# Product-key expert stage of a two-layer trunk: 0.9 dots a tile and less of the other tokens' top-k between the gathers' begin and the gates

## The chip, the cores and the metric

The kernel runs on one core of a Trainium2 chip. The metric is device time in microseconds (us) of one execution, from repeated runs: before the change the median of three is 1582.73 us (1582.06 to 1584.29). A profiled execution of the same kernel took 1584.51 us, of which the span from the first to the last instruction is 1582.6 us. Engines are named as in the profile: PE multiplies matrices, DVE and ACT work on vectors, POOL (GpSimd) here issues row gathers, and SP issues most weight transfers.

## What is computed

Two layers run one after the other on 256 tokens of width 1024. Each mixes tokens (convolution, windowed attention, spatial gating) and then retrieves experts; the change lies in the second part, which for one layer is this:

```python
q = (t @ w_pq).reshape(T, PEER_HEADS, 2, PEER_HALF)
s = jnp.einsum('thpk,hpnk->thpn', q, sub_keys, preferred_element_type=jnp.float32)
top_s, top_i = lax.top_k(s, PEER_TOPK)
...
best_s, best_pos = lax.top_k(cand_s.reshape(T, PEER_HEADS, PEER_TOPK * PEER_TOPK), PEER_TOPK)
experts = jnp.take_along_axis(...)
gate = jax.nn.softmax(best_s, axis=-1)
u = expert_down[experts]
act = jax.nn.gelu(jnp.einsum('td,thkd->thk', t, u, ...), approximate=False)
wgt = (gate * act).astype(t.dtype)
vv = expert_up[experts]
return jnp.einsum('thk,thkd->td', wgt, vv)
```

There are 8 heads with 16 picks each, so 128 picks a token, among 16384 experts in each of the two tables (down and up), float32 throughout. The scale and shift of each norm come from a modulation, a product of one vector with a 1024 by 6144 matrix for each layer.

## The kernel before

**Two ways for the tokens.** Most tokens (168 in layer 0, 160 in layer 1) are dense: they are multiplied with every expert, in 128 tiles of 128 experts, first all of the down table and then all of the up table. The gate values are put into a dense array and multiply the activations. The other tokens (88 and 96) are sparse: for pick slot k, one indirect DMA by POOL (a gather) fetches 128 rows of 4 KB, one to a partition, of the down table, and DVE forms the 128 dot products at once (`dot(k)`, line 1084). Later the same is done with the rows of the up table (`add_row`, line 1099).

**The down loop** (in `experts`, lines 1239 to 1347) is a loop over tiles i = 0 to 127; "T38" below is the tile i = 38 of one layer. A tile's matmuls (`chunk_mm`, line 357) are 16 on PE, and its weights are one transfer of 512 KB into one of seven `raw` buffers. Even tiles' transfers are issued from ACT's queue (kind "second"), the others from SP's. Fifteen tiles, from T4 on, are loaded ahead into parts of the array `arena` that `AHEAD_AT` lists. After its matmul such a part can be lent to gathers as a row buffer.

**Order.** From here on the instructions stand in the order in which the program writes them (manual_schedule), on each engine. An engine works through its own list in order, so an instruction whose data is missing holds up all that stands behind it. In each tile, behind the matmuls, the program writes: the use of gates, the gelu of the tile pair on ACT (line 1150), the gate factors on ACT (`factors`, lines 1117 to 1123), a one-hot comparison on DVE (`compare`, line 1107), and then what the change touches:

- `run_fill(budget)` runs pieces of the top-k on DVE, each with a cost that was written by hand. The queue `fills[1]` belongs to the half of the tokens that holds the sparse ones, and `fills[0]` to the other half. When `fills[1]` is done, its picks are known, and this tile is `begin`. Three tiles later the gathers start, two a tile.
- When `fills[0]` is done (its last piece of work is `gate`, lines 922 to 924), two tiles later `to_picks` lets PE transpose the result (line 934), ACT copies it (lines 939 to 942), and one tile after that DVE forms the remainder (line 943) and `compare` runs for the first two gate groups. The next tile is `start`: ACT's `factors` for both groups are written there. From `start + FLUSH` tiles on PE multiplies the groups (`gate_mm`, line 1133), spread up to tile 124.
- Dots are written from `begin + D_FIRST` on at a rate a tile: `DOT_SLOW` while pieces are left in `fills[0]`, `DOT_FAST` from then to `start`, `DOT_RATE` afterwards. A dot frees its row buffer, and the next gather is written at once behind it (`fetch`). As many gathers are open as there are row buffers.
- `run_aside` multiplies one chunk of the next modulation on DVE (line 227). Six such chunks wait in buffers from tile 19 on.

In words, `passing` holds the lent parts of `arena` which the activations of later tiles will overwrite. Once `fills[0]` is down to `RETIRE` pieces they are not lent again.

Of the kernel before, what the change touches and what calls it, by code (L numbers as in the profile page):

```python
# [46 lines left out]
WHERE_LAG = 3  # L47
SETS_LAG = 6
SETS_KNOWN = 22
D_FIRST = 8  # L50
DOT_SLOW = 0.3
DOT_RATE = (0.85, 0.92)
DOT_FAST = 1.6
RETIRE = 9
AHEAD_AT = (8, 12, 16, 36, 40, 44, 48, 52, 56, 60, 64, 68, 100, 28, 32)
KEPT = 100
FLUSH = 6
# [8 lines left out]
FILL_DOWN = (2.2, 2.1)  # L66
# [16 lines left out]
def hybrid_trunk(ctx: ExitStack, tc: tile.TileContext, x_in, c_in, vec_in, w_ada, w_in, w_out, w_pq,  # L83
# [45 lines left out]
    def region(at, *shape):  # L129
        n = 1  # L130
        for s in shape:
            n *= s
        v = flat[:, at:at + n]
        if len(shape) == 2:
            v = v.rearrange("p (a b) -> p a b", b=shape[1])
        elif len(shape) == 3:
            v = v.rearrange("p (a b c) -> p a b c", b=shape[1], c=shape[2])
        return v
# [78 lines left out]
    fills = deque(), deque()  # L217

    def run_fill(budget):
        Src.credit = min(budget, Src.credit + budget)  # L220
        while (fills[0] or fills[1]) and Src.credit > 0:
            cost, fn = (fills[1] or fills[0]).popleft()
            fn()
            Src.credit -= cost
# [63 lines left out]
    def run_aside(least=4):  # L288
        if Src.asides and Src.asides[0][0] <= Src.cast - least:
            Src.asides.popleft()[1]()  # L290
# [29 lines left out]
    for layer in range(DEPTH):  # L320
# [3 lines left out]
        if layer == 0:  # L324
# [5 lines left out]
            n = len(head)  # L330
# [677 lines left out]
    def experts(layer, rest):  # L1008
# [59 lines left out]
        def fetch():  # L1068
            while free and len(held) < min(2 * TS, known_to[0]) and quota[0] > 0:
                quota[0] -= 1  # L1070
                n = len(held)
                k = n % TS
                held[n] = free.popleft()
                nc.gpsimd.indirect_dma_start(  # L1074
                    out=held[n], out_offset=None, in_=rows if n >= TS else down_rows[:, :],
                    in_offset=bass.IndirectOffsetOnAxis(ap=R_WHERE[:, k:k + 1].bitcast(U32), axis=0))
# [144 lines left out]
        begin = None  # L1221
# [12 lines left out]
        for i in range(128):  # L1234
# [32 lines left out]
                known_to[0] = SETS[0][1]  # L1267
                fetch()
            if start is None:
                run_fill(FILL_DOWN[layer] if begin is None else FILL_DOWN[layer] - 1.2 * DOT_SLOW)  # L1270
            if known:
                known_at.append((i + PICKS_LAG, known.pop()))
                if begin is None:
                    begin = i
# [14 lines left out]
            elif start is not None and i >= start + FLUSH:  # L1289
# [3 lines left out]
                while sent < want and not waiting:  # L1293
                    waiting.append((sent, gate_mm(sent)))
                    sent += 1
                    make = True
            if not retired and begin is not None and len(fills[0]) <= RETIRE:
                retired.extend(passing)
                for row in [row for row in free if any(row is r for r in passing)]:
                    free.remove(row)  # L1300
            n = i - AHEAD_FIRST
            if 0 <= n < len(AHEAD_AT) and AHEAD_AT[n] >= 28:
                assert not retired
                free.append(region(AHEAD_AT[n] * S, D))
                if AHEAD_AT[n] != KEPT:
                    passing.append(free[-1])
                fetch()
            if begin is not None:
                if i == begin + SETS_LAG:
                    spread_rest()  # L1310
                if i == begin + SETS_KNOWN:
# [4 lines left out]
                    fetch()  # L1316
                if i >= begin + D_FIRST:
                    due += DOT_RATE[layer] if start is not None else DOT_SLOW if fills[0] else DOT_FAST
                if start is not None and i < start + FLUSH:
# [28 lines left out]
    for layer in range(DEPTH):  # L1348
        hh = split_halves()
        update, late = mixing(layer, qg, update, late)  # L1350
        rest = retrieval(layer, update, late)
        update, late, qg = experts(layer, rest)
# [85 lines left out]
```

## Time and profile before

| | |
|---|---|
| median of three runs | 1582.73 us (1582.06 to 1584.29) |
| profiled execution | 1584.51 us |
| its span | 1582.6 us |
| PE busy | 1542.3 us (97%) |
| DVE busy | 1000.0 us (63%) |
| ACT busy | 472.5 us (30%) |
| POOL busy | 496.8 us (31%) |
| moved by DMA | 571.21 MB, mean 361 GB/s |
| mean clock granted to PE | 0.991 |

The times are microseconds from the start of the span. A busy time counts overlapping instructions once; two instructions on the same engine can overlap a little, since the next one starts before the last one has drained. In the profile's rows of time, a figure in square brackets is the idle time of the engine just before, and behind the arrow stands what ended it. In rows by windows, each engine has its busy time and, in brackets, the number of its instructions; then follow the clock granted to PE (1.00 is full), the share of time in which the DMA engines were busy (slightly over 1 when they are full) and the GB/s that they moved.

### The profile page before, as it was taken

To read this page: it belongs to the slowest core of one execution; us is meant where nothing else is said; L and a number is where in the kernel's file an instruction comes from. 1 tells how busy PE (TensorE), PEld (TensorE's weight loads), DVE (VectorE), ACT (ScalarE), POOL (GpSimd) and SP (SyncE) were. 2 spreads that over 40 slices of the span, in tenths; PEclk is the share of its full clock that TensorE was granted. 3 is DMA by queue.
4 is the path that set the end of the run, shared out by engine and by line. 5 is a ranking of instruction groups with operands and counts; after the bars stand their busy time and mean duration, and the time that the engine had idled before them with its cause. 6 is when DMAs were issued, how large, how long until landed. Compare 5 with 4: busy or idle time off the path is not lost.

```text
span 1582.6 us, 28957 instructions
## 1 busy us (share of the span) xinstructions
PE 1542.3 (97%) x11240; PEld 1505.1 (95%) x11240; DVE 1000.0 (63%) x2255; ACT 472.5 (30%) x1356; POOL 496.8 (31%) x424
## 2 busy tenths in 40 slices
PE   6999999999999999998999999999999999999997
PEld 5879999999999999998999899999999999999997
DVE  6778898677787444444337578877667754444434
ACT  2346313465553000000026663134656610000000
POOL 1000124334344434444200001245443334444441
PEclk9999999999999999999999999999999999999998
DMA  9998489999999999999955574899999999999995
GB/s 385 339 375 319 138 289 348 418 418 419 417 418 416 415 419 419 418 419 419 412 189 171 186 258 139 292 351 419 417 418 419 418 419 419 418 419 419 419 418 211
DMA packets 156681, 571.21 MB, mean 361 GB/s; under 512 B 18131, under 2 KB 18659, under 8 KB 155392
## 3 DMA queue, kind: packets, MB, share of 16 engines
q1 hardware_dynamic: 66096, 241.07, 39.7%
q0 software_dynamic: 55744, 202.36, 32.0%
q10 hardware_dynamic: 34704, 125.93, 19.9%
q8 instruction: 88, 1.44, 0.3%
q14 instruction: 49, 0.40, 0.1%
HBM read 564.02 MB, written 4.09 MB: 359 GB/s over the span
## 4 chain that ended last, share of the span: by engine, by line
PE 40%; DMA 38%; issue 8%; DVE 7%; POOL 4%; ACT 2%; ACTq 0%; POOLq 0%; SPq 0%; DVEq 0%
DMA arena<-in_up,arena 17%; PE acc L1173 17%; DMA arena<-in_down_rows,arena 12%; PE ch L357 9%; DMA spots<-in_down_rows,arena 3%; DMA raw<-in_up 3%; POOL arena L1074 3%; PE ch L359 2%; PE ch L360 2%; PE ch L361 2%; DVE raw L227 1%; DMA raw<-in_w_ada 1%; PE ch L446 1%; DVE arena L1084 1%; PE g L952 1%
## 5 line engine op out<-in xcount | busy, mean ns | idle before, releaser
L1173 PE MATMUL acc<-arena,raw 128*128 128x168 f32 (+1 forms) x4096 | 580.5, 305 | 9.0 <-DMA raw<-in_up 9.0
L1173 PEld LDWEIGHTS acc<-arena,raw 128*128 128x128 f32 x4096 | 577.6, 192 | 11.3 <-DMA raw<-in_up 11.2
L357 PE MATMUL ch<-arena,raw 128*128 128x168 f32 (+2 forms) x3776 | 560.7, 307 | 0.1
L357 PEld LDWEIGHTS ch<-arena,raw 128*128 128x128 f32 x3776 | 536.2, 190 | 5.6 <-issue 1.8
L1099 DVE SCALAR_TENSOR_TENSOR spots<-arena,spots 128x1024 f32<-128x1024 f32 x156 | 200.4, 1284 | 222.1 <-DMA arena<-in_up,arena 220.8
L1074 POOL DMA_INDIRECT arena<-in_up,arena x159 | 215.1, 1353 | 280.5 <-DMA arena<-in_up,arena 203.9
L1074 POOL DMA_INDIRECT arena<-in_down_rows,arena x151 | 178.3, 1181 | 242.9 <-DVE arena L1084 180.7
L1084 DVE SCALAR_TENSOR_TENSOR arena<-arena,spots 128x1024 f32<-128x1024 f32 x151 | 183.1, 1222 | 86.1 <-DMA arena<-in_down_rows,arena 79.6
L1117 ACT ACTIVATE arena<-arena,parts 128x128 f16<-128x128 f16 x164 | 64.6, 394 | 142.1 <-DVE arena L1107 102.5
L388 ACT ACT_TABLE_LOAD x6 | 7.7, 1283 | 284.9 <-PE acc L1173 284.8
L357 PE MATMUL ch<-arena 128*128 128x160 f32 (+2 forms) x544 | 86.0, 317 | 6.1 <-issue 3.6
L357 PEld LDWEIGHTS ch<-arena 128*128 128x128 f32 x544 | 79.8, 192 | 11.2 <-ACT arena L410 5.2
L1150 ACT ACTIVATE arena<-ch 128x336 f32<-128x336 f32 (+32 forms) x122 | 41.9, 343 | 149.4 <-PE ch L357 128.9
L227 DVE SCALAR_TENSOR_TENSOR aside<-aside,arena 128x1024 f32<-128x1024 f32 x48 | 58.6, 1220 | 43.9 <-DMA aside<-in_w_ada 43.8
L359 PE MATMUL ch<-hh,hi 128*128 128x256 f32 x288 | 82.6, 289 | 2.0 <-DVE arena L477 1.9
L360 PE MATMUL ch<-hh,lo 128*128 128x256 f32 x288 | 81.8, 284 | 0.0
L361 PE MATMUL ch<-hh,hi 128*128 128x256 f32 x288 | 81.7, 284 | 0.0
L270 DVE TENSOR_TENSOR lo<-raw,hi 128x1024 fp32r<-128x1024 f32 x42 | 51.2, 1225 | 37.3 <-ACT hi L277 36.3
L227 DVE SCALAR_TENSOR_TENSOR raw<-raw,arena 128x1024 f32<-128x1024 f32 x48 | 57.9, 1217 | 8.9 <-DMA raw<-in_w_ada 5.4
L1119 ACT ACTIVATE arena<-arena,parts 128x128 f16<-128x128 f16 x164 | 63.4, 387 | 0.0
L1123 ACT ACTIVATE arena<-arena,parts 128x128 f16<-128x128 f16 x164 | 63.4, 386 | 0.0
L1121 ACT ACTIVATE arena<-arena,parts 128x128 f16<-128x128 f16 x164 | 63.4, 386 | 0.0
(231 smaller groups left out, 1661.9 us busy)
## 6 DMA issues: line engine op xcount, KB each, us to landing
raw<-in_up SPq DMA_DIRECT2D x128, 512.0 KB
raw<-in_up ACTq DMA_DIRECT2D x128, 512.0 KB
raw<-in_down SPq DMA_DIRECT2D x114, 512.0 KB
raw<-in_down ACTq DMA_DIRECT2D x112, 512.0 KB
raw<-in_w_ada SPq DMA_DIRECT2D x48, 512.0 KB
aside<-in_w_ada SPq DMA_DIRECT2D x48, 512.0 KB
raw<-in_w_pq SPq DMA_DIRECT2D x32, 512.0 KB
arena<-in_down SPq DMA_DIRECT2D x30, 512.0 KB
```

The costliest lines, as they stand in the source:

```text
L227: nc.vector.scalar_tensor_tensor(raw, raw, 1.0, cact, op0=OP.mult, op1=OP.mult, accum_out=mods[layer][:, col:col + 1])
L357: nc.tensor.matmul(dst, hi[:, cols], k[0], start=start, stop=stop, **kw)
L359: nc.tensor.matmul(dst, hi[:, cols], k[0], start=start, stop=False, **kw)
L360: nc.tensor.matmul(dst, lo[:, cols], k[0], start=False, stop=False, **kw)
L361: nc.tensor.matmul(dst, hi[:, cols], k[1], start=False, stop=stop, **kw)
L1074: nc.gpsimd.indirect_dma_start(out=held[n], out_offset=None, in_=rows if n >= TS else down_rows[:, :], in_offset=bass.IndirectOffsetOnAxis ...
L1084: nc.vector.scalar_tensor_tensor(row, row, 1.0, R_DX[which(k)[0]], op0=OP.mult, op1=OP.mult, accum_out=R_DOTS[:, k:k + 1])
L1099: nc.vector.scalar_tensor_tensor(R_SUM[s], row, w, R_SUM[s], op0=OP.mult, op1=OP.add)
L1117: nc.scalar.activation(og[0][:, 0, i, :], oh[:, 0, i, :], AF.Copy, scale=parts[:, 0, t + i:t + i + 1])
L1119: nc.scalar.activation(og[1][:, 0, i, :], oh[:, 0, i, :], AF.Copy, scale=parts[:, 1, t + i:t + i + 1])
L1121: nc.scalar.activation(og[0][:, 1, i, :], oh[:, 1, i, :], AF.Copy, scale=parts[:, 0, t + 2 + i:t + 3 + i])
L1173: nc.tensor.matmul(acc[d // 2][:, (d % 2) * S:(d % 2) * S + T], u[:, d * P:(d + 1) * P], acts[:, i, :], start=i == 0 and d % 2 == 0, stop= ...
```

## The change

Five places differ. Dots may start one tile earlier (`D_FIRST`) and come at 0.9 instead of 0.3 a tile while `fills[0]` has pieces. Up to that tile, `run_fill` gets its full budget, and from it on 1.2 times 0.9 less. When `fills[0]` is empty, one modulation chunk a tile is multiplied instead. `RETIRE` falls from 9 to 4, and the two lent parts 28 and 32 are not lent any more.

```diff
-D_FIRST = 8
-DOT_SLOW = 0.3
+D_FIRST = 7
+DOT_SLOW = 0.9
...
-RETIRE = 9
+RETIRE = 4
...
             if start is None:
-                run_fill(FILL_DOWN[layer] if begin is None else FILL_DOWN[layer] - 1.2 * DOT_SLOW)
+                if begin is None or i < begin + D_FIRST:
+                    run_fill(FILL_DOWN[layer])
+                elif fills[0]:
+                    run_fill(FILL_DOWN[layer] - 1.2 * DOT_SLOW)
+                else:
+                    run_aside()
...
-            if 0 <= n < len(AHEAD_AT) and AHEAD_AT[n] >= 28:
+            if 0 <= n < len(AHEAD_AT) and AHEAD_AT[n] >= 36:
```

By the loop's rules, `begin` stays at T11 in layer 0 and T12 in layer 1. The last piece of `fills[0]` moves from T30 to T36 (layer 0) and from T32 to T39 (layer 1), `start` from T34 to T40 and from T36 to T43, and the first gate product from T40 to T46 and from T42 to T50. At the end of the down loop both kernels have written the same dots (88 and 96) and the same gathers, and the up loop is unchanged.

**First place: DVE, layer 0, from the end of the other tokens' top-k to the first comparisons.** L1084 is a dot, L922 to L924 are `gate`, L943 follows the copies of the picks, L1107 is `compare`, L227 a modulation chunk. Before:

```order
L1084 SCALAR_TENSOR_TENSOR arena<-arena,spots 128x1024
L922 TENSOR_REDUCE arena<-arena 128x8
L923 RECIPROCAL arena<-arena 128x8
L924 TENSOR_TENSOR arena<-arena 128x128
L1084 SCALAR_TENSOR_TENSOR arena<-arena,spots 128x1024 x5
L943 SCALAR_TENSOR_TENSOR parts<-g,arena 128x128
L1107 TENSOR_TENSOR arena<-iota_85,picks 128x1024 x2
```

The same place now:

```order
L1084 SCALAR_TENSOR_TENSOR arena<-arena,spots 128x1024 x2
L922 TENSOR_REDUCE arena<-arena 128x8
L923 RECIPROCAL arena<-arena 128x8
L924 TENSOR_TENSOR arena<-arena 128x128
L1084 SCALAR_TENSOR_TENSOR arena<-arena,spots 128x1024
L227 SCALAR_TENSOR_TENSOR aside,mod_112<-aside,arena 128x1024
L1084 SCALAR_TENSOR_TENSOR arena<-arena,spots 128x1024 x2
L227 SCALAR_TENSOR_TENSOR aside,mod_112<-aside,arena 128x1024
L1084 SCALAR_TENSOR_TENSOR arena<-arena,spots 128x1024 x2
L227 SCALAR_TENSOR_TENSOR aside,mod_112<-aside,arena 128x1024
L943 SCALAR_TENSOR_TENSOR parts<-g,arena 128x128
L1107 TENSOR_TENSOR arena<-iota_85,picks 128x1024 x2
```

Counted from 0 in each layer, the last dot ahead of `gate` was dot 2 and is now dot 15; the last dot ahead of the first comparison was dot 7 and is now dot 20.

**Second place: DVE, layer 1, the same stretch.** Before:

```order
L1084 SCALAR_TENSOR_TENSOR arena<-arena,spots 128x1024
L922 TENSOR_REDUCE arena<-arena 128x8
L923 RECIPROCAL arena<-arena 128x8
L924 TENSOR_TENSOR arena<-arena 128x128
L1084 SCALAR_TENSOR_TENSOR arena<-arena,spots 128x1024 x3
L1063 TENSOR_SCALAR arena<-pairs 128x32
L1084 SCALAR_TENSOR_TENSOR arena<-arena,spots 128x1024 x2
L943 SCALAR_TENSOR_TENSOR parts<-g,arena 128x128
L1107 TENSOR_TENSOR arena<-iota_85,picks 128x1024 x2
```

The same place now:

```order
L1084 SCALAR_TENSOR_TENSOR arena<-arena,spots 128x1024 x2
L922 TENSOR_REDUCE arena<-arena 128x8
L923 RECIPROCAL arena<-arena 128x8
L924 TENSOR_TENSOR arena<-arena 128x128
L1084 SCALAR_TENSOR_TENSOR arena<-arena,spots 128x1024
L227 SCALAR_TENSOR_TENSOR aside,mod_112<-aside,arena 128x1024
L1084 SCALAR_TENSOR_TENSOR arena<-arena,spots 128x1024 x2
L227 SCALAR_TENSOR_TENSOR aside,mod_112<-aside,arena 128x1024
L1084 SCALAR_TENSOR_TENSOR arena<-arena,spots 128x1024
L227 SCALAR_TENSOR_TENSOR aside,mod_112<-aside,arena 128x1024
L943 SCALAR_TENSOR_TENSOR parts<-g,arena 128x128
L1107 TENSOR_TENSOR arena<-iota_85,picks 128x1024 x2
```

Here the last dot ahead of `gate` was dot 2 and is now dot 17, and the last one ahead of the first comparison was dot 7 and is now dot 21. In layer 0 the factors of the first two groups stand on ACT in T40, ahead of the gelu of the pair T40 and T41; before, in T34, ahead of the gelu of T34 and T35. In layer 1 they stand in T43, behind the gelu of T42 and T43. The transposes of the picks (PE, L934) come behind the matmuls of T38 in layer 0 and T41 in layer 1; before, behind T32 and T34.

## Prediction

> **What bounds the kernel now.** I read the windows first, then what PE waits for, then PE, DVE, POOL and ACT in order of time around the stretch that changes. The windows (columns: PE, PEld, DVE, ACT, POOL, clock, DMA share, GB/s):
>
> ```profile
> 240.00:250.00 10.00, 10.00 (x72) 10.00 (x72) 9.65 (x21) 2.42 (x4) 7.93 (x8) 1.00 0.86 222
> 260.00:270.00 10.00, 10.00 (x73) 10.00 (x72) 3.04 (x6) 1.64 (x6) 0.00 (x0) 1.00 1.03 417
> 320.00:360.00 40.00, 40.00 (x317) 39.64 (x317) 28.34 (x58) 23.05 (x80) 15.97 (x14) 1.00 1.03 418
> 520.00:560.00 40.00, 40.00 (x283) 40.00 (x282) 17.73 (x18) 0.00 (x0) 15.49 (x13) 1.00 1.03 419
> 680.00:720.00 40.00, 38.41 (x267) 37.86 (x267) 19.07 (x19) 0.00 (x0) 16.54 (x12) 1.00 1.03 419
> 720.00:760.00 40.00, 33.27 (x206) 32.51 (x205) 19.16 (x21) 0.00 (x0) 16.41 (x14) 0.91 1.03 419
> 1050.00:1060.00 10.00, 10.00 (x76) 10.00 (x75) 3.20 (x7) 1.78 (x6) 2.42 (x3) 1.00 1.03 418
> 1400.00:1440.00 40.00, 40.00 (x297) 40.00 (x296) 17.28 (x14) 0.00 (x0) 19.96 (x14) 1.00 1.03 418
> ```
>
> From 260 us in layer 0 and 1050 us in layer 1 on, the transfers run at 417 to 419 GB/s, and no row shows more: that is the ceiling here, 524,288 bytes (a tile's weights, or one gather) in 1.25 us. PE is full as well. Both bind, and which one sets the end differs by place:
>
> ```profile
> PE acc L1173 <- DMA raw<-in_up: 9.0, 7, 3.5
> PE acc L1179 <- DVE spots L1099: 4.5, 1, 4.5
> PE g L1133 <- ACT arena L1117: 1.9, 2, 1.3
> L1173 PE MATMUL acc<-arena,raw 128*128 128x168 f32 x983 | 140.5, 306 | 0.0
> L1173 PE MATMUL acc<-arena,raw 128*128 128x160 f32 x1475 | 200.5, 299 | 0.0
> ```
>
> The last two rows are from stretches without waits: a matmul starts every 140.5 / 983 = 0.143 us in layer 0 and every 200.5 / 1475 = 0.136 us in layer 1, so a tile of 16 takes 2.29 and 2.18 us. In layer 0's up loop PE waits for weights: the windows at 680 and 720 us have 16 and 77 fewer matmuls than that at 520 us, 93 x 0.143 = **13.3 us**, the slow clock included. Layer 1 waits at its very end, for the sums over gathered rows (L1179). So both layers end on bytes. A later PE costs nothing there until these reserves are used up.
>
> **The change: where dots will wait.** Total work on every engine stays; only its order changes. In layer 1, before, DVE (dots are L1084, here dots 12, 17 and 18; L922 to L924 end the top-k; L943 precedes the comparisons):
>
> ```profile
> 1045.46 0.28 DVE L922 TENSOR_REDUCE arena<-arena 128x8 f32<-128x128 f32 x1
> 1046.01 0.29 DVE L924 TENSOR_TENSOR arena<-arena 128x128 f32<-128x128 f32 x1
> 1058.91 0.29 DVE L943 SCALAR_TENSOR_TENSOR parts<-g,arena 128x128 f32<-128x128 f32 x1 [6.80 <-ACT picks L942]
> 1066.38 1.23 DVE L1084 SCALAR_TENSOR_TENSOR arena<-arena,spots 128x1024 f32<-128x1024 f32 x1 [0.25 <-DMA arena<-in_down_rows,arena]
> 1081.18 1.22 DVE L1084 SCALAR_TENSOR_TENSOR arena<-arena,spots 128x1024 f32<-128x1024 f32 x1 [1.74 <-DMA arena<-in_down_rows,arena]
> 1083.69 1.22 DVE L1084 SCALAR_TENSOR_TENSOR arena<-arena,spots 128x1024 f32<-128x1024 f32 x1 [1.28 <-DMA arena<-in_down_rows,arena]
> ```
>
> From dot 12 to 17 each waited for its gather: 14.8 us for five, 2.96 us apart, 1.36 tiles. The change asks for 0.9 dots a tile, which is more than arrive. Would earlier issue make them arrive sooner? POOL's issues of gathers 15 and 16 in layer 0, and DVE's dots 15, 16 and 20 there:
>
> ```profile
> 256.27 1.08 POOL L1074 DMA_INDIRECT arena<-in_down_rows,arena  x1 [0.65 <-issue]
> 270.76 1.14 POOL L1074 DMA_INDIRECT arena<-in_down_rows,arena  x1 [13.40 <-DVE parts L943]
> 283.09 1.22 DVE L1084 SCALAR_TENSOR_TENSOR arena<-arena,spots 128x1024 f32<-128x1024 f32 x1 [1.78 <-DMA arena<-in_down_rows,arena]
> 285.91 1.23 DVE L1084 SCALAR_TENSOR_TENSOR arena<-arena,spots 128x1024 f32<-128x1024 f32 x1 [1.59 <-issue]
> 299.35 1.22 DVE L1084 SCALAR_TENSOR_TENSOR arena<-arena,spots 128x1024 f32<-128x1024 f32 x1 [1.20 <-DMA arena<-in_down_rows,arena]
> ```
>
> Issued 14.5 us apart, they were used 2.8 us apart. The gathers' queue never ran dry, though POOL stood for 13.4 us. So I take the arrivals of before as those of after: gather 17 of layer 1 at 1081.2 us, gathers 15 and 20 of layer 0 at 283.1 and 299.3.
>
> Now what stands behind these dots. PE in order of time (L934 is the picks' transposes, L1133 the first gate product):
>
> ```profile
> 269.03 18.41 PE L357 MATMUL ch<-arena,raw 128*128 128x168 f32 x128
> 287.27 0.63 PE L1133 MATMUL g<-arena 128*128 128x128 f16 x8
> 1057.41 0.49 PE L934 MATMUL g<-ident,arena 128*128 128x128 f32 x3
> 1057.74 17.55 PE L357 MATMUL ch<-arena,raw 128*128 128x160 f32 x128
> 1075.13 0.62 PE L1133 MATMUL g<-arena 128*128 128x128 f16 x8
> ```
>
> *Layer 1, the transposes.* The first gate stands behind T42, so T41 ends at 1075.1 - 2.18 = 1072.9. The transposes now stand there and need L922 to L924 (0.84 us), which stand behind dot 17: 1081.2 + 1.15 + 0.84 = 1083.2. **PE waits 10.3 us.** Before, this work was done at 1046.3, 11 us ahead of its transposes: that cover is gone. Bounds: dot 14 came at 1066.4 + 2 x 2.96 = 1072.3; if the waiting PE left all transfers to gathers, three more rows would land by 1076.1, and the wait would be 5.2 us. I take 10.3, since weights already asked for are served first or alongside.
>
> *Layer 0, the transposes.* T38 ends two tiles ahead of 287.3, at 282.7. Dot 15 and 0.84 us end at 285.1: 2.4 us.
>
> *Layer 0, the comparisons.* They stand behind dot 20, one modulation chunk (1.15) and L943 (0.2); the first ends at 299.3 + 1.15 + 1.15 + 0.2 + 0.64 = 302.5. ACT in layer 0 before, the first of two groups' factors and the gelu behind the last:
>
> ```profile
> 271.86 0.39 ACT L1117 ACTIVATE arena<-arena,parts 128x128 f16<-128x128 f16 x1
> 276.54 0.43 ACT L1150 ACTIVATE arena<-ch 128x336 f32<-128x336 f32 x1
> ```
>
> Sixteen factors take 4.7 us. The gelu of T40 and T41 stands behind them, so it is done at 302.5 + 4.7 + 0.4 = 307.6. T44 needs its PSUM buffer (two for tile pairs). T43 ends at 282.7 + 2.4 + 5 x 2.29 = 296.6: **PE waits 11.0 us.** With the transposes, layer 0 is 13.4 us late. Lower bound: by the loop's rules the gate product behind T50 now needs dots up to 27, and needed dots up to 22. Five more rows at 1.25 us are 6.3 us that PE has to give up even if nothing else goes wrong.
>
> *Layer 1, the comparisons.* Behind dot 21. Gathers were quick after PE's wait at 1083, so I put four rows at 2 us: 1083.2 + 8 and 3.9 us of DVE work, 1095; factors 4.7: 1100. T48 would start at 1072.9 + 10.3 + 6 x 2.18 = 1096 plus the slow clock below, 1098: some 2 us.
>
> **What is given back.** PE's tail, and layer 0's folds for comparison:
>
> ```profile
> 810.33 6.58 PE L1179 MATMUL acc<-fold,spots 128*128 128x64 f32 x48
> 1565.67 6.61 PE L1179 MATMUL acc<-fold,spots 128*128 128x32 f32 x30 [4.51 <-DVE spots L1099]
> 1565.00:1570.00 5.00, 4.33 (x21) 4.33 (x21) 0.61 (x1) 0.00 (x0) 0.00 (x0) 0.53 0.00 0
> 1080.46 4.56 PE L357 MATMUL ch<-arena,raw 128*128 128x160 f32 x32
> 1088.44 5.74 PE L357 MATMUL ch<-arena,raw 128*128 128x160 f32 x32
> 1075.59 4.56 PE L357 MATMUL ch<-arena,raw 128*128 128x160 f32 x32
> 1094.02 0.62 PE L1133 MATMUL g<-arena 128*128 128x128 f16 x8
> ```
>
> - Layer 0: 13.4 us late against 13.3 us of waiting for weights. While PE stands, the weight buffers fill up and gathers land, and the up loop starts with these in hand. The end is set by bytes, and they flow on. **0 us.** If the cover fails, up to the whole 13.4.
> - Layer 1's own wait of before: 1075.59 to 1080.46 is 4.9 us for two tiles and a gate; 1080.46 to 1088.44 took 8.0 and 1088.44 to 1094.02 5.6, so 3.8 us, that go, because the gates start eight tiles later: -3.8.
> - The tail: if PE is at least 4.5 us late and the transfers are not, the wait of 4.5 us goes, and the folds run at full clock: 48 took 6.58 us in layer 0, so 30 should take 4.1 instead of 6.6. -4.5 and -2.5.
> - A long wait brings the slow clock (0.53 behind the last one). The 2.5 us just found is its price once; I take 2 us for layer 1's long wait.
>
> The Trainium skill, "TensorE: Matmul & The Clock Gate", Part 1, says that PE drops to half clock after about 3.4 us of idling and needs about 3.4 us of work to return. By that each of the two long waits would cost 1.7 us more (an estimate from that page); the trace, with 0.53 behind a wait of 4.5 us, agrees, and the sum would move by -0.3 us, since layer 0's share stays inside its reserve.
>
> **Sum.** Layer 0: 0. Layer 1: 10.3 + 2 + 2 - 3.8 - 4.5 - 2.5 = +3.5; PE thus arrives 10.5 us late at folds that waited 4.5. Against it: the transposes' wait lies anywhere between 5.2 and 10.3, and the middle is 2.5 less. I take **+2 us**, near the upper end, as the trace's weights and gathers shared transfers in every stretch. The profiled execution (span 1582.6, in all 1584.5) becomes span 1584.6 and 1586.5 in all. It stands 1.8 us above the median of the runs, 1582.73, so the median of after is 1584.7; I say **1584.5 us**.
>
> **Rivals.**
>
> *Slower by more.* ACT is the place. While it stands at the factors, the even tiles' weights queued behind on it aren't issued either; half of the weight stream dries up during 11 us, and gathers alone have only six free rows. If the transfers fall below the ceiling for that stretch, bytes are lost for good, and layer 0 returns only part: with half of 13.4 lost, +6.7, and layer 1 at its upper sum, +3.5: 1593. It decides from the point where under about half of 419 GB/s is moved there. For it: POOL and ACT both stand in order. Against it: SP's weights and six gathers make 4 to 5 us of transfers at any moment.
>
> *Faster.* Gathers get all the transfers when PE stands. Layer 1's transposes wait 5.2 us, and the 2 us at T48 go: PE is 10.5 - 5.1 - 2 = 3.4 us late at the folds and meets sums that are ready at 4.5 or a little sooner, since the last weights are asked for later. The sum is then 3.5 - 5.1 - 2 = -3.6 if they are sooner, and -2.5 if not: 1579.1 to 1580.2. The Trainium skill, "DMA: Bandwidth & Descriptors", "Queues, rings and completion order", has each DMA engine take turns between the queues that hold work, so that a gather's share grows only when a weight queue is empty. By that rule the truth lies between this rival and my sum. The equal spacing above agrees with it.
>
> *The change doesn't do what it says:* dots at 0.9 a tile may be written but not executed, since arrivals give about 0.74. That is part of my forecast.
>
> **How the numbers follow.** A measurement of this kernel can tell 0.2%, 3.2 us, from no change. My forecast, 1584.5 with its own range 1580 to 1586: 0.46. The slower rival, and milder forms of it from 1586 up: 0.37. The faster rival and stronger forms of it, 1574 to 1580: 0.17, nearly all of it under 1579.5. The range 1578 to 1594 leaves out about 0.1 on each side. Faster 0.16, same 0.47, slower 0.37.
>
> **What would show it.** Right: waits of PE at L934 of about 10 us near 1073 and 2 us near 283; a PE wait of about 11 us for ACT's gelu (L1150) behind T43 of layer 0; fewer lost matmuls at 680 to 760 us; no wait at L1179; DMA at 418 GB/s throughout. Wrong: dots 15 to 20 that arrive much earlier than 283 to 299 us, DMA below 400 GB/s between 290 and 310 us, or layer 0's up loop still losing 13 us.

## The result and the profile after

The changed kernel takes 1603.26 us (median of four runs, 1601.96 to 1605.55) against 1583.09 us for the kernel before on the same chip (1582.06 to 1584.29): ratio 1.0129, 95% interval 1.0111 to 1.0146. It is **20 us slower**; 1584.5 was forecast, with a range of 1578 to 1594. The profiled execution has a span of 1601.0 us, 18.4 more than before.

Where the 18.4 us lie is read from the times at which tiles begin: the first matmul of each tile in the two traces, one subtracted from the other.

| stage, us | before | after | difference |
|---|---|---|---|
| start to T0, layer 0 | 188.8 | 189.5 | +0.7 |
| layer 0, T0 to T40 | 96.1 | 97.9 | +1.8 |
| T40 to T52 | 30.5 | 35.9 | +5.4 |
| T52 to T120 | 174.7 | 172.6 | -2.1 |
| T120 to the up loop | 19.3 | 27.0 | +7.7 |
| layer 0's up loop | 314.3 | 314.2 | -0.1 |
| layer 1, T0 to T40 | 91.7 | 91.2 | -0.5 |
| T40 to T52 | 33.0 | 38.6 | +5.6 |
| T52 to T120 | 165.4 | 166.8 | +1.4 |
| T120 to the up loop | 18.8 | 27.3 | +8.5 |
| layer 1's up loop | 292.6 | 282.6 | -10.0 |

There is one trace a kernel. In the kernels below that leave layer 0's down loop as it was, T0 to T40 took 94.5 to 98.7 us, T52 to T120 172.6 to 175.4, and the stretch behind T120 always 19.3. Layer 0's up loop took 311.1 to 316.0 us in all kernels that leave it as it was. Differences within these bounds say nothing.

Three things stand out: waits around T40 in both layers, a second loss behind T120 in both layers, and an up loop of layer 0 that gives nothing back. PE's waits of the changed kernel (time in all, times, longest):

```profile
PE acc L1173 <- DMA raw<-in_up: 9.1, 7, 3.4
PE ch L357 <- ACT arena L1150: 5.0, 1, 5.0
PE g L1133 <- ACT arena L1117: 4.9, 7, 0.9
PE g L934 <- DVE arena L912: 4.9, 1, 4.9
PE g L934 <- DVE arena L924: 3.6, 1, 3.6
```

The wait at L1179 is gone. The waits for weights (L1173) are what they were, 9.1 us for 9.0. In order of time PE reads, at T44 of layer 0, at the picks of layer 1, and at the end of layer 0's down loop:

```profile
285.14 11.57 PE L357 MATMUL ch<-arena,raw 128*128 128x168 f32 x80
301.71 8.78 PE L357 MATMUL ch<-arena,raw 128*128 128x168 f32 x48 [5.00 <-ACT arena L1150]
...
1085.90 0.27 PE L934 MATMUL g<-ident,arena 128*128 128x128 f32 x1
1091.07 0.47 PE L934 MATMUL g<-ident,arena 128*128 128x128 f32 x1 [4.89 <-DVE arena L912]
1095.18 0.47 PE L934 MATMUL g<-ident,arena 128*128 128x128 f32 x1 [3.63 <-DVE arena L924]
1095.44 22.21 PE L357 MATMUL ch<-arena,raw 128*128 128x160 f32 x144
...
506.88 2.52 PE L357 MATMUL ch<-arena,raw 128*128 128x168 f32 x16
509.24 0.32 PE L1133 MATMUL g<-arena 128*128 128x128 f16 x2
510.20 1.11 PE L1133 MATMUL g<-arena 128*128 128x128 f16 x6 [0.65 <-ACT arena L1117]
511.15 2.50 PE L357 MATMUL ch<-arena,raw 128*128 128x168 f32 x16
514.53 0.52 PE L1133 MATMUL g<-arena 128*128 128x128 f16 x2 [0.89 <-ACT arena L1117]
515.69 1.11 PE L1133 MATMUL g<-arena 128*128 128x128 f16 x6 [0.64 <-ACT arena L1117]
```

The last six rows show the second loss. By the loop's rules the 42 groups of layer 0 now begin at T46 and not at T40, one to an even tile, and so there is no room for the last: groups stand on T122, 123, 124 and 125 (in layer 1 too). On following tiles each comparison (DVE), its factors (ACT) and its product (PE) wait for the ones before. From 500 us on, with all dots done, the transfers run dry too:

```profile
500.00:510.00 10.00, 9.49 (x74) 8.89 (x73) 5.84 (x11) 7.31 (x28) 0.00 (x0) 1.00 0.91 345
510.00:520.00 10.00, 7.96 (x43) 6.67 (x44) 2.96 (x6) 4.21 (x16) 0.00 (x0) 0.84 0.35 108
520.00:530.00 10.00, 10.00 (x71) 10.00 (x70) 6.20 (x6) 0.45 (x1) 4.73 (x5) 0.99 0.74 224
```

Before, 510 to 520 us moved 401 GB/s. Against 418 GB/s, 5.8 MB were not moved in these 30 us, 13.8 us at the ceiling. POOL's rows for the seventh gather of up rows tell why; after, and then before:

```profile
522.22 0.94 POOL L1074 DMA_INDIRECT arena<-in_up,arena  x1 [27.73 <-PE ch L357]
```

```profile
508.76 0.94 POOL L1074 DMA_INDIRECT arena<-in_up,arena  x1 [4.05 <-PE ch L357]
```

Six up rows are gathered ahead. The next goes where the tokens of the dense matmuls lie, and waits for the last of these. The last dot starts at 492.05 us now, 31 us ahead of the up loop (before at 502.27, 7 us ahead), so the rows are full early, and the weights move only as fast as PE frees their buffers: 27.7 us of POOL's idle time instead of 4.1.

### The profile page after: what moved, and what is told of

The parts are those of the page before. It is cut to its first block, busy times and chain, and to the rows that moved or that the text cites. A ratio compares the mean times of both kernels' runs of the same rounds, so it can differ in the third digit from the quotient of the medians.

```text
span 1601.0 us, 28956 instructions
## 1 busy us (share of the span) xinstructions
PE 1547.4 (97%) x11240; PEld 1508.0 (94%) x11240; DVE 999.5 (62%) x2248; ACT 471.1 (29%) x1353; POOL 484.7 (30%) x424
## 3 DMA queue, kind: packets, MB, share of 16 engines
q10 hardware_dynamic: 34704, 125.93, 19.8%
## 4 chain that ended last, share of the span: by engine, by line
PE 62%; DMA 24%; DVE 6%; ACT 3%; issue 2%; POOL 1%; ACTq 0%; SPq 0%; DVEq 0%; POOLq 0%
PE acc L1173 29%; PE ch L357 18%; DMA arena<-in_down_rows,arena 11%; DMA raw<-in_up 8%; DMA spots<-in_down_rows,arena 2%; PE ch L359 2%; PE ch L360 2%; PE ch L361 2%; PE g L1133 1%; POOL arena L1074 1%; DMA raw<-in_w_ada 1%; PE ch L446 1%; PE g L952 1%; DVE raw L227 1%; PE acc L357 1%
## 5 line engine op out<-in xcount | busy, mean ns | idle before, releaser
L1173 PE MATMUL acc<-arena,raw 128*128 128x168 f32 (+1 forms) x4096 | 577.8, 304 | 9.1 <-DMA raw<-in_up 9.1
L1173 PEld LDWEIGHTS acc<-arena,raw 128*128 128x128 f32 x4096 | 575.2, 191 | 11.1 <-DMA raw<-in_up 10.9
L357 PE MATMUL ch<-arena,raw 128*128 128x168 f32 (+2 forms) x3776 | 567.3, 310 | 5.8 <-ACT arena L1150 5.0
L357 PEld LDWEIGHTS ch<-arena,raw 128*128 128x128 f32 x3776 | 542.7, 192 | 11.6 <-ACT arena L1150 5.3
L1074 POOL DMA_INDIRECT arena<-in_up,arena x159 | 202.8, 1276 | 307.4 <-DMA arena<-in_up,arena 118.0
L1084 DVE SCALAR_TENSOR_TENSOR arena<-arena,spots 128x1024 f32<-128x1024 f32 x153 | 185.8, 1222 | 89.3 <-DMA arena<-in_down_rows,arena 82.6
L227 DVE SCALAR_TENSOR_TENSOR aside<-aside,arena 128x1024 f32<-128x1024 f32 x48 | 58.7, 1222 | 115.3 <-DMA aside<-in_w_ada 115.3
L1150 ACT ACTIVATE arena<-ch 128x320 f32<-128x320 f32 (+39 forms) x126 | 44.5, 354 | 209.8 <-PE ch L357 187.8
L1143 DVE SCALAR_TENSOR_TENSOR arena<-arena,g 128x200 f32<-128x200 f32 (+20 forms) x82 | 42.5, 518 | 45.6 <-ACT arena L1141 42.8
```

Of the source, the lines that this page charges most:

```text
L227: nc.vector.scalar_tensor_tensor(raw, raw, 1.0, cact, op0=OP.mult, op1=OP.mult, accum_out=mods[layer][:, col:col + 1])
L357: nc.tensor.matmul(dst, hi[:, cols], k[0], start=start, stop=stop, **kw)
L1074: nc.gpsimd.indirect_dma_start(out=held[n], out_offset=None, in_=rows if n >= TS else down_rows[:, :], in_offset=bass.IndirectOffsetOnAxis ...
L1084: nc.vector.scalar_tensor_tensor(row, row, 1.0, R_DX[which(k)[0]], op0=OP.mult, op1=OP.mult, accum_out=R_DOTS[:, k:k + 1])
L1173: nc.tensor.matmul(acc[d // 2][:, (d % 2) * S:(d % 2) * S + T], u[:, d * P:(d + 1) * P], acts[:, i, :], start=i == 0 and d % 2 == 0, stop= ...
```

## The experiments

Each run is given by its median less that of the kernel before on the same chip, with the ratio's interval. Stage times are from the traces as above, beside 320.6 us (layer 0's down loop), 314.3 (its up loop), 308.9 and 292.6 (layer 1's).

**Which part, which layer.** Only the rate back at 0.3:

```diff
-DOT_SLOW = 0.9
+DOT_SLOW = 0.3
```

> The changed kernel with DOT_SLOW back at 0.3; the other parts stay (full budget up to begin + 7, modulation chunks between the last piece and start, RETIRE 4, two lent parts fewer). Gates begin at T40 and T42 as before the change. If the rate of 0.9 makes the loss, this is the time of before: 1583 us (1581 to 1586), without waits of PE at L934 and behind T43. If fewer lent parts, RETIRE or the modulation chunks have a share, it stands above 1587. Where the rate accounts for everything, the difference to the changed kernel is about 20 us.

Measured: +0.3 us (0.9990 to 1.0012). At the old rate the other edits (`D_FIRST`, `RETIRE`, the lent parts, the chunk behind the last piece) cost nothing that can be seen; the 20 us come from the rate and what it moves.

```diff
-DOT_SLOW = 0.9
+DOT_SLOW = (0.9, 0.3)
...
-    run_fill(FILL_DOWN[layer] - 1.2 * DOT_SLOW)
+    run_fill(FILL_DOWN[layer] - 1.2 * DOT_SLOW[layer])
...
-    due += DOT_RATE[layer] if start is not None else DOT_SLOW if fills[0] else DOT_FAST
+    due += DOT_RATE[layer] if start is not None else DOT_SLOW[layer] if fills[0] else DOT_FAST
```

> The changed kernel with the rate 0.9 in layer 0 alone, 0.3 in layer 1. By the stages of the two traces layer 0's part is +12.8 us in the down loop and 0 in the up loop, layer 1's +14.8 and -10.0: 1583 + 13 = 1596 us (1593 to 1598), with layer 0's up loop at 314 us. FLOW (the prediction's step for layer 0): 1583 to 1586, with the up loop 10 us shorter.

> The changed kernel with the rate 0.9 in layer 1 alone, 0.3 in layer 0. By the stages of the two traces layer 1's part is +14.8 us in its down loop and -10.0 in its up loop: 1583 + 5 = 1588 us (1586 to 1590). By the prediction's sum for layer 1: 1585. With layer 0 alone (15.5 us) it should add up to the changed kernel's 20.6.

Layer 0 alone: **+15.5 us** (1.0084 to 1.0118), down loop 333.5, up loop 314.0. Layer 1 alone, with (0.3, 0.9): **+2.6** (1.0002 to 1.0022), down 321.8, up 282.7. The sum, 18.1, is near the 20.2 of the whole. Layer 1 came out near the prediction's number (+3.5, taken as +2), though not by its terms (see below). The error of the sum lies in layer 0.

Between the two rates:

> The changed kernel with 0.6 dots a tile. Gates begin at T42 and T44 (before T40 and T42, changed T46 and T50), and only two groups stand on following tiles at the end of layer 0's down loop, none in layer 1. If the loss sets in where more dots are asked for than arrive (0.74 a tile in the trace of before): 1583 (1581 to 1585). If it grows with the tiles by which gates begin later and the dots that stand ahead: a third to a half of 20 us, 1590 to 1593.

Measured: +2.0 us (0.9996 to 1.0020); both expectations miss by their numbers. PE does wait (3.4 us in layer 0 and 5.5 in layer 1 between T42 and T52), but nothing crowds in layer 1, and its up loop gives 4.7 us back. The loss isn't in proportion to the rate.

**Two causes apart.** Dots at 0.9 but picks early, so that the gates begin at T38; then the reverse, gates six tiles later with dots and picks as before:

```diff
-                if begin is None or i < begin + D_FIRST:
+                if begin is None or i < begin + D_FIRST or fills[0]:
...
-FLUSH = 6
+FLUSH = 12
```

> The changed kernel with the full top-k budget kept until fills[0] is empty: the dots stand at 0.9 a tile as in the change, but the other tokens' picks are ready early, and the gates begin at T38 in both layers and end at T121 without crowding. Theory LATE GATES (the loss comes from the late begin of the gates and the four crowded last groups): 1583 (1580 to 1586). Theory DOTS AHEAD (comparisons and picks wait for dots that are written faster than their gathers arrive, wherever the gates stand): dot 23 is now ahead of the comparisons of T40, and was there at 308.6 us where T40 began at 285, so that PE waits some 20 us in layer 0, of which only gates and a few small waits give any back: 1595 to 1603.

> The kernel before with FLUSH 12 for 6: gates begin six tiles later, as after the change, and the last ones crowd on T122 to T125 (layer 0) and T122 to T124 (layer 1); dots, picks and top-k stand as before. Theory ROOM: layer 0 6.4 us longer and nothing returned in its up loop; layer 1 some 5 us of crowding, less 3.8 us of the wait at 1080 to 1090 us that goes and less part of the 4.5 us wait for the folds: together 1589.5 us (1587 to 1592). Theory FLOW: layer 0 even, layer 1 even: 1583.

The first: +7.8 us (1.0036 to 1.0069), between the two theories. Dots ahead of the comparisons do cost, here in layer 1:

```profile
1054.25 12.71 PE L357 MATMUL ch<-arena,raw 128*128 128x160 f32 x80
1074.73 8.72 PE L357 MATMUL ch<-arena,raw 128*128 128x160 f32 x48 [7.78 <-ACT arena L1150]
```

but little is lost behind T120 (19.6 us for 19.3 in layer 0, 21.2 for 18.8 in layer 1), and without late gates the other 12 us of the change are missing. The second: **+13.2 us** (1.0064 to 1.0098), more than expected. Behind T120 of layer 0 it took 28.3 us for 19.3, much as in the changed kernel (27.0). The part that was not expected is that the third group's comparison is written behind the first gate, so with later gates it too stands behind more dots: PE waited 7.8 us for its factors in layer 1, at 1107 us. Late gates alone, without a faster rate, thus make both kinds of wait.

The crowd taken away, in both layers and then in layer 0 alone:

```diff
-                if want < NG and i % 2:
+                if want < NG and i % 2 and want < sent + 2:
```

> The changed kernel, but a gate group may also be multiplied on an odd tile once two are due. The last four groups then no longer stand on four tiles in a row (T122 to T125), where PE waited for ACT's factors (L1117) in both layers; one extra group each stands near T73 and T99 in layer 0, T65 and T95 in layer 1. Theory ROOM (the crowded last groups cost PE about 6.4 us in layer 0 and 6.0 us in layer 1, and layer 0 gives nothing back, since its row buffers are full at the end of the down loop whatever PE does): 1603.3 - 12.4 = 1591 us, both down loops 6 us shorter, and layer 0's up loop still 314 us with about 9 us of waits for weights. Theory FLOW (the step of the prediction: what PE loses in layer 0's down loop comes back in its up loop): only layer 1's part counts, 1597. Rival ACT (factors are late anyway, the wait only moves to the odd tiles): 1603.

> The changed kernel with the rate 0.9 in layer 0 alone and an extra gate group on an odd tile when two are due. Against layer 0 alone (15.5 us): if the crowded last groups cost what the two traces show at the end of layer 0's down loop (24.8 against 19.3 us behind T120, so 5 to 6), and the two odd tiles cost 2, it is 3 to 4 us faster, 1595 to 1596. If the crowd is a symptom only (PE would stand anyway until bytes come): 1599.

In both layers: +15.0 us (1.0073 to 1.0132; runs from 1592.7 to 1602.4), some 5 less than the change, not the 12 of ROOM, and the two intervals overlap. The stretches behind T120 are back at 19.8 and 18.9 us, but an extra group on an odd tile costs too: at 1150 us of layer 1 PE waited 1.5 and 0.65 us and ran at the slow clock (14 matmuls in 3.8 us, for 1.9). In layer 0 alone: +11.9 (1.0050 to 1.0086) against 15.5 (1.0084 to 1.0118), the 3 to 4 us expected, though the intervals just touch.

**Is there a reserve in layer 0?** Extra matmuls behind T60, whose result is not used; first 72 calls, then 36:

```diff
+            if layer == 0 and i == 60:
+                extra = bank("acc", 4)
+                for _ in range(72):
+                    nc.tensor.matmul(extra[:, :T], R_HX[:, 0, :P], R_HX[:, 0, :T], start=True, stop=True, skip_group_check=True)
```

> The kernel before with 72 extra matmuls of a dense tile's kind on PE behind T60 of layer 0 (72 x 0.143 = 10.3 us; their result is not used). No other engine's order changes. Theory ROOM: the end moves by nearly all of it, 1593 us (1591 to 1595): layer 0's down loop is 10.3 us longer, its up loop keeps 314 us and its 9 us of waits for weights, and the transfers fall below 418 GB/s at the change from down to up loop. Theory FLOW: the up loop gets 10 us shorter and the waits for weights nearly vanish: 1583 (1582 to 1585).

> The kernel before with 36 extra calls of a matmul on PE behind T60 of layer 0's down loop, which the run before showed to be two passes each: 72 passes of 0.143 us, 10.3 us (there 144 passes took 20.7 us and the kernel 13.9 us more). Theory CLOCKED (nine or so up rows are gathered ahead, and the next gather waits for the last matmul of the down loop, so that layer 0's up loop takes 312 to 316 us from whenever it begins): the end moves by 7 to 10.3 us, 1590 to 1593, and the up loop stays within 2.5 us of 314. Theory FLOW (bytes bind, a late PE is returned): 1583 to 1584.

A call of this kind stands in the trace as two matmuls (144 rows for 72 calls), so the first run put in 20.7 us: +13.9 (1.0074 to 1.0107). The second put in 10.4: **+6.3** (1.0029 to 1.0050), a little under what was expected. Its up loop is 314.2 us; what is saved (some 2 to 4 us) is saved inside the down loop. Its windows behind the extra work, which ran from 336.2 to 346.4 us, and a row each of POOL and DVE there:

```profile
340.00:350.00 10.00, 10.00 (x77) 9.96 (x76) 3.53 (x7) 0.97 (x4) 1.28 (x2) 1.00 0.83 340
350.00:360.00 10.00, 10.00 (x81) 9.91 (x80) 7.11 (x16) 6.11 (x23) 3.56 (x3) 1.00 0.90 313
360.00:370.00 10.00, 10.00 (x81) 9.91 (x80) 7.98 (x15) 6.08 (x23) 5.24 (x4) 1.00 0.98 370
```

```profile
350.09 0.94 POOL L1074 DMA_INDIRECT arena<-in_down_rows,arena  x1 [7.54 <-DVE arena L1084]
...
347.52 0.41 DVE L1143 SCALAR_TENSOR_TENSOR arena<-arena,g 128x240 f32<-128x240 f32 x1 [6.17 <-ACT arena L1141]
```

That is the flaw of "bytes flow on". When the gates of PE are late, the weight buffers fill, DVE stands at the use of a gate (L1143, 6.17 us), the dots behind it free no row, and POOL has nowhere to gather to (7.54 us). At T44 of the changed kernel no gate is in use yet, and there the transfers went on (418 GB/s at 280 to 300 us). Counting the transfers of each trace that ended between T0 and the begin of the up loop, 236 rows of 512 KB were moved before, 238 with layer 0 alone at 0.9 and 238 here. In the 12.9 us by which the down loop of layer 0 alone is longer, ten rows could move at 1.25 us each; two were carried over.

The same work inside the up loop, where the sums on DVE use nothing that PE makes; the second run, on the identity, was:

```diff
+                if layer == 0 and i == 30:
+                    extra = bank("ch", 2)
+                    for _ in range(48):
+                        nc.tensor.matmul(extra[:, :P], ident, ident, start=True, stop=True, skip_group_check=True)
```

> The same 10.3 us of extra matmuls on PE, in layer 0's up loop ahead of its tile 30. Theory CLOCKED: here gathers and sums go on while PE is busy, so the waits of PE for weights (9.0 us, 13.3 us with the slow clock) shrink by the 10.3 us: 1583 to 1585, with under 3 us of waits for weights. If PE's lost time is paid anywhere in layer 0, whatever the place: 1593.

> As the run before with extra matmuls in layer 0's up loop ahead of tile 30, but on the identity, whose place no gather overwrites (there the extra work first waited 11.3 us for a gathered row, so PE stood for 22 us and not 10.3): 48 calls of two passes of 0.11 us, 10.6 us. Theory CLOCKED (from the begin of the up loop on, bytes set its end): the waits for weights, 9.0 us and 13.3 with the slow clock, take the 10.6 us up: up loop 314 to 317 us, time 1583 to 1586. If PE's lost time is paid wherever it lies: 1594.

The first tells little: its operand had been lent to a gather, and PE first waited 11.3 us and then worked 12.0 (+16.4). The second put in 10.9 us and took **+6.8** (1.0031 to 1.0059), up loop 321.0: some 60% are paid even here. CLOCKED, too, falls with its number. The short waits before 700 us went; those at 720 to 760 us stayed (7.2 us at T96, T99 and T101 of the up loop, where the kernel before has 6.7).

**What holds the up loop.** The queues of the kernel before from 540 to 680 us (packets, MB, share of 16 engines):

```profile
q0 software_dynamic: 5836, 21.26, 37.2%
q1 hardware_dynamic: 5831, 21.22, 37.1%
q10 hardware_dynamic: 4398, 15.99, 28.0%
```

Gathers (q0) and SP's queue (q1) have the same share to 0.2%; ACT's (q10) carries only its half of the weights. The Trainium skill, "DMA: Bandwidth & Descriptors", "Queues, rings and completion order", has each DMA engine take turns between the queues that hold work; these rows agree. SP's queue has the other half of the weights, 18 modulation chunks, and at tiles 89 and 102 the next layer's tables (1.4 MB) and x_dram (1 MB), with weights behind them. Could that be the wait?

```diff
-            if kind == "second":
+            if kind == "second" or kind == "aside" and Src.aside % 2 and Src.starts[0] + 150 < Src.loaded < Src.starts[1]:
...
-                    nc.sync.dma_start(X.rearrange("p a b -> p (a b)"), x_dram)
+                    nc.scalar.dma_start(X.rearrange("p a b -> p (a b)"), x_dram)
```

> The kernel before; in layer 0's up loop every second modulation chunk's transfer, and in both layers the reload of x_dram, are issued from ACT's queue instead of SP's. In the trace of before SP's queue moves 5.8 rows of 512 KB in 20 us all through this loop, gathers 5.8 and ACT's queue 4.3; SP carries half of the weights (20 / 2.29 / 2 = 4.4 rows), 18 chunks, and at 720 and 756 us the 1.4 MB of tables and the 1 MB of x_dram. Theory SHARE (PE waits for weights at 680 to 760 us because SP's queue has more to carry than its share, not because bytes lack as a whole): most of the 13.3 us goes, up loop 301 to 307 us, time 1571 to 1577. Theory BYTES (the loop lacks bytes as a whole, as the prediction had it): the gathers get fewer, the same waits come from them or from ACT's weights, 1583.

> The same edit of the queues on the changed kernel. SHARE: layer 0's up loop is shortened by as much as in the kernel before, so 1603 - (7 to 12) = 1591 to 1596: the waits for weights hang on what SP's queue carries at tiles 89 and 102 of the up loop, and not on when PE arrives. BYTES: 1603.

On the kernel before: -3.2 us (0.9957 to 0.9995), up loop 310.1, a third of what SHARE said. On the changed kernel: +15.2 beside the kernel before (1.0080 to 1.0128), up loop 308.0; the 5 us less than the change are not clear of noise, since the two intervals overlap. The waits themselves tell more. Without this edit both kernels wait at T75, T79, T96 and T101, though PE reaches these tiles 15 us later in the changed one; with it the wait at T96 falls from 3.5 to 1.0 us and from 3.4 to 0.8, and the first two go (T101's stays). They change by the queues, in both kernels alike, and not by PE's arrival.

T99 and T101 wait for weights in SP's queue: those of T99 were issued at 723.40 us, behind the tables, and landed at 744.2. T96 is another matter, since its weights are ACT's:

```profile
709.30 0.33 SPq L213 DMA_DIRECT2D aside<-in_w_ada  x1
725.85 0.34 ACTq L254 DMA_DIRECT2D raw<-in_up  x1
```

In the trace both transfers signal on the same semaphore. ACT's issue stood until SP's modulation chunk had landed, at 725.75 us, and PE then waited for these weights until 734.75. So what stood in SP's queue held up ACT's too. The reload of x_dram has no part in the waits of the kernel before: it was issued at 755.56 us, behind the last of them. Then the two loads later:

```diff
-                if i == 56 * S // T + 4 and layer + 1 < DEPTH:
+                if i == 110 and layer + 1 < DEPTH:
...
-                if i == 64 * S // T + 5:
+                if i == (112 if layer == 0 else 64 * S // T + 5):
```

> The kernel before with every second modulation chunk of layer 0's up loop issued from ACT's queue, and in layer 0 the loads of the next layer's tables (1.4 MB) moved from tile 89 to 110 and the reload of x_dram (1 MB) from tile 102 to 112, where the gathers come to their end and the transfers fell to 341 and 187 GB/s. Theory SHARE (the waits hang on what SP's queue carries while gathers take their share): the waits of 720 to 760 us, 7.4 us in the run before, go too; up loop 300 to 305 us, time 1571 to 1576. Theory BYTES: the waits only move to other tiles, 1580 to 1583.

> The tables and x_dram later as in the run before this one, all chunks left on SP's queue. SHARE: the waits at 720 to 760 us shrink, those near 680 to 700 us (1.6 us) stay, since SP's weights and chunks alone are a little over its share: 1575 to 1579. If the two loads have no part in these waits: 1583.

Measured: -3.4 us (0.9963 to 0.9988) with half of the chunks on ACT's queue, -3.3 (0.9965 to 0.9992) without; 310.3 and 311.3 us. Both miss SHARE's numbers. Windows of the second:

```profile
740.00:760.00 20.00, 20.00 (x141) 19.81 (x140) 9.18 (x10) 0.00 (x0) 8.51 (x6) 1.00 1.03 419
760.00:780.00 20.00, 20.00 (x143) 20.00 (x142) 7.17 (x6) 0.00 (x0) 6.40 (x6) 1.00 1.03 418
780.00:800.00 20.00, 15.41 (x95) 14.90 (x94) 7.77 (x7) 1.58 (x2) 0.05 (x1) 0.91 0.91 365
```

PE had 104 matmuls at 740 to 760 us before, and has 141 now; the hole is at 780 to 800 us, behind the loads, which SP now issued at 763 to 768 us (T119 and T121 wait, 1.0 and 3.6 us). The waits follow the loads. Last, the loads at their old tiles, but in the gathers' queue, and half of the chunks on ACT's:

```diff
-        q = nc.gpsimd if layer == 0 else nc.sync
+        q = nc.gpsimd
...
-                    nc.sync.dma_start(X.rearrange("p a b -> p (a b)"), x_dram)
+                    (nc.gpsimd if layer == 0 else nc.sync).dma_start(X.rearrange("p a b -> p (a b)"), x_dram)
```

> The kernel before with every second modulation chunk of layer 0's up loop on ACT's queue, and the tables and x_dram (2.4 MB) of layer 0 at their old tiles, but issued from POOL into the gathers' queue. Theory SHARE (PE's waits follow these loads because they stand ahead of weights in SP's queue): no weights stand behind them now, the gathers come 4.6 rows later, which at 5.8 rows in 20 us is 16 us, and they had 27 us left; the waits for weights fall under 3 us, up loop 300 to 306 us, time 1571 to 1577. Theory BYTES: PE waits for weights or for the sums as long as before, 1580 to 1584.

Measured: **+3.9 us** (1.0011 to 1.0032), up loop 316.4, outside the numbers of both theories. PE, and DVE's last sum there:

```profile
703.03 96.03 PE L1173 MATMUL acc<-arena,raw 128*128 128x168 f32 x672 [0.58 <-DMA raw<-in_up]
...
807.46 9.55 PE L1179 MATMUL acc<-fold,spots 128*128 128x8 f32 x44 [8.05 <-DVE qg L535]
...
806.12 1.28 DVE L1099 SCALAR_TENSOR_TENSOR spots<-arena,spots 128x1024 f32<-128x1024 f32 x1 [1.22 <-DMA arena<-in_up,arena]
```

96 us without a wait for weights, and 2.0 us of such waits in the whole loop: what SP's queue carried was what made PE wait, directly or through ACT's issue. But the gathers came later by what was put ahead of them (last sum at 806.1 us, before at 795.7), and PE stood 8 us at the folds. Two limits lie within a few us of each other, the weights behind SP's loads and the gathers' end, and both count from the begin of the loop.

**Gathers ahead of POOL's long stand.** An attempt at the kernel before itself:

```diff
-SETS_LAG = 6
+SETS_LAG = 10
```

> The kernel before with SETS_LAG 10 for 6: the write and reload of the pairs through DRAM (L1050 to L1059), on which POOL stood from 1018.6 to 1032 us, comes behind 16 gathers instead of 8. Of the transfers of 1028 to 1048 us, 10.8 of 16 rows of 512 KB were moved there. If the eight more gathers fill that gap, five rows or 6 us of layer 1's transfers come earlier, and the wait of 4.5 us for the sums at the end goes: 1576 to 1580. If POOL then stands longer behind the queued gathers and the queue runs dry after them: 1583 or more.

Measured: +8.1 us (1.0038 to 1.0072). Layer 1's T0 to T40 took 103.3 us for 91.7, and mostly not for the reason in the expectation; see the last section.

## Why the prediction was wrong, by its steps

- **The step that failed: "Layer 0: 13.4 us late against 13.3 us of waiting for weights ... they flow on. 0 us."** Layer 0 alone costs 15.5 us, and its up loop is 314 us as before. The waits for weights were read as spare transfers. They hang on what SP's queue carries, and are met at the same tiles however late PE comes. And bytes don't flow on to the end. At T44 they did, but what they brought early could not be kept: six up rows ahead (not the nine of an expectation above), seven weight buffers and DVE's order behind gate uses hold no more, and the transfers ran dry ahead of the up loop. The prediction's own test ("layer 0's up loop still losing 13 us") came true.
- **Left out: the last groups.** The first gate was foreseen at T46 and T50, but not that 42 and 40 groups on even tiles then don't end by T122. The stretches behind T120 are 7.7 and 8.5 us longer; of these the extra groups' own products are about 1.5 (three of 0.47 us) and the waits for factors 2.2 and 2.8. Part of the rest is the slow clock (0.84 at 510 to 520 us; two tiles in 6.45 us for 4.6).
- *The lateness of layer 0: 13.4 us.* Its down loop is 12.8 us longer, but that agreement is luck: 5.4 come at T40 to T52 and 7.7 behind T120.
- *Layer 1, the transposes: 10.3 us.* PE stood from 1086.1 to 1095.4, 9.3 us (its waits were 8.5; 7.5 to 10.5 in the other three traces with this rate in layer 1). Right, and the slow clock behind it too (0.76 at 1080 to 1100 us; nine tiles in 22.2 us, 2.6 more than at 2.18 each). No wait followed at T48.
- *Layer 0, transposes and comparisons: 2.4 and 11.0 us.* Place and chain of the second were right, the sizes not: none and 5.0 us. In the other four traces with these tiles the transposes waited 0 to 5.5 us and the gelu 2.1 to 6.4, together 6.4 to 7.6, half of the 13.4. Dot 15 began at 278.3 us and not 283.1, dot 20 at 293.3 and not 299.3, so arrivals did come sooner with gathers issued sooner, against the step "I take the arrivals of before". With the slow clock 6.9 us were lost behind T43, of which nothing came back.
- *What layer 1 gives back: 3.8, 4.5 and 2.5 us.* Right in kind: nothing waits at L1133 near 1100 us or at L1179. But the up loop gives back 10.0 us, where 4.5 and 2.5 were counted. That its sum came out close is in part luck: the run with layer 1 alone lost 5.7 us behind T120, which were left out, and the 2 us counted for T48 didn't come.
- *The slower rival* had the sign, not the mechanism: DMA moved 418 and 419 GB/s at 280 to 320 us, where ACT stood. It fell at 500 to 530 us, at the change of loops.

What stays open is the exact split between waits around T40 and the late, crowded gates: 7.8 us remained with dots ahead alone and 13.2 came with late gates alone, but the two aren't independent, since late gates also put comparisons behind more dots. The fastest kernels here are those with the two loads later or spread over queues, 3.2 to 3.4 us faster than the kernel before; the change was tried with one of these edits only, and stays slower.

## What to carry to other kernels

A wait for data late in a loop isn't a reserve for an earlier delay until it is clear which queue, which tile and which issue it hangs on: move it, or put idle work in, and see whether it stays. Transfers go on during a stall only as far as free buffers and the order of every other engine allow; count the buffers before counting on the bytes. And where a start moves by some tiles, follow the schedule to its last item: what no longer fits crowds at the end.

## What was not expected of the hardware

With 16 gathers issued in a row (`SETS_LAG` 10), PE's matmuls on weights that are loaded ahead stood apart one by one, with nothing that the profile shows:

```profile
1020.87 0.30 PE L357 MATMUL ch<-arena 128*128 128x160 f32 x1 [1.72 <-issue]
1022.29 0.36 PE L357 MATMUL ch<-arena 128*128 128x160 f32 x1 [1.13 <-issue]
1024.44 0.42 PE L357 MATMUL ch<-arena 128*128 128x160 f32 x1 [1.79 <-issue]
```

Such waits were 10.9 us in twelve places there and 3.6 us in five in the kernel before. From 1005 to 1040 us, where most of layer 1's lie, the gathers' queue took 68% of the engines' time (49% in the kernel before). The clock behind them was slow as well (0.74 at 1020 to 1040 us). What PE waited for was not tried.
